# The mixer's weight halves made by GpSimd, and the stick-breaking mask made in VectorE's running product instead of by a matmul

## The chip, the cores and the metric

The kernel runs on one core of a Trainium2 chip. The metric is the device time of one execution in microseconds (us). The time given for a kernel is the median of its runs. A profiled execution gives a trace of every instruction, from which the views of the profile are drawn.

## The reference, cut to what matters

One layer of a streaming encoder, on 1024 tokens of width 1024, in float32: a half feed-forward block, a token mixer, and a second half feed-forward block, each between two RMS norms with shift, scale and gate. The change lies in the mixer, and there in its stick-breaking branch (8 heads of dimension 64) and in the projections that feed both of its branches:

```python
proj = u @ w_in                      # q, k, v of both branches, gate_A, gate_B
z = einsum('bhqd,bhkd->bhqk', qi, k) * scale
before = spos[None, :] < ti[:, None]                      # key strictly earlier than query
log_fail = where(before, log_sigmoid(-z), 0.0)
later = cumsum(log_fail, axis=3, reverse=True) - log_fail  # sum over keys between s and t
w = where(before, exp(log_sigmoid(z) + later), 0.0)
ya = einsum('bhqk,bhkd->bhqd', w, v)
```

So a key's weight is sigmoid(z) times the product of sigmoid(-z) over all later keys that are still before the query, and 0 for keys that are not before it.

## The kernel before, in words

**Split arithmetic.** Every large product is made of three TensorE matmuls in a rounded float32 format: high by high, high by low and low by high halves. The high half of an operand is a rounded copy by ScalarE, the low half is the difference of operand and high half. For a mixer weight the helper `split` (L135 to L143) does this: a DMA on SyncE's queue brings 128x1024 weights into `raw` (two buffers), ScalarE copies them to `wsH` (L141), and an engine that the caller can choose, VectorE by default, subtracts (L142) to give `wsL`. Of `wsH` and `wsL` there are four buffers each.

**The mixer's two parts.** The stick-breaking branch has four units `u` = 0 to 3, each with two heads (`par` = 0, 1), and each head has four steps `j`. A step treats two query blocks of 128 rows, `qb` = 2j and 2j+1. Block `qb` sees L = 128(qb+1) keys, so the blocks of a head are 128, 256, ... 1024 keys long. One head of four steps is called a round below: eight rounds in all. Units 4 to 7 are the four heads of the differential branch, with softmax in place of the running product.

**A step of the stick-breaking branch** (`sb_weights`, L996 to L1013). For each block and each piece of up to 512 keys: TensorE makes z by two matmuls (`qk`, L938 and L939) and, on the piece that holds the diagonal, a third one (L1005) that adds a 128x128 bfloat16 mask (0 below the diagonal, -1e30 from it on) by way of an identity matrix. ScalarE then writes sigmoid(z) to `be` (L1006) and sigmoid(-z) to `f` (L1007). VectorE runs the product backwards over the whole of `f` in one scan (L1010) and multiplies `be` by `f` one column further on (L1011). Of `f` there are two buffers, of `be` four.

**Weights times values** (`av`, L946 to L985, and `sb_out`). TensorE transposes 128x128 blocks of `be` through PSUM (L955, L956), ScalarE takes the high half `tH` (L960, L963, L965), VectorE the low half `tL` (L961, L964, L966), and TensorE multiplies both with v (L1021) into the bank `pav`. This is done for a step while the next step's z, `be` and `f` are being made.

**Filler work.** Between those pieces TensorE works on projections: classes `QJob`, `KJob`, `VJob` and `GateJob`, 48 matmuls each, a V job 192 (L813, L815, L817), dealt out by `fill` in equal shares. `advance_` (L923) loads the weights of the first two jobs of the list ahead of need (`Job.load`, L800 to L802, which calls `split`); a `VJob` needs two weight tiles and is loaded and run through where it stands (L1194). K jobs also copy their halves to the other half of the partitions on GpSimd (L866, L867), four pairs a job, which is all that GpSimd does in the mixer.

**The order.** The program is written in the order above; a list scheduler of the framework then places the instructions on the engines, by its own estimate of times. Each engine works through its list strictly in order: an instruction that waits for a semaphore holds up everything behind it on that engine.

Of the kernel before, what the change touches and what calls it, by code (L numbers as in the profile page):

```python
# [14 lines left out]
BF16 = mybir.dt.bfloat16  # L15
AF = mybir.ActivationFunctionType
ALU = mybir.AluOpType
# [3 lines left out]
P = 128  # L21
# [8 lines left out]
NEG = -1e30  # L30
# [16 lines left out]
def build(ctx, tc, A, out):  # L47
# [714 lines left out]
    pending = ffn("wg1", "wu1", "wd1", start0, pending0, steps1, lambda c: 2 if c == 1 else 5 if c < 10 else 0, steps1b, 0, lambda t: A["x"][t * P:(t + 1) * P, :], lambda t: h_dram[0][t])  # L762

    pending = mixer(locals())

    ffn("wg2", "wu2", "wd2", start_half, pending, lambda fp, psum: mod_gate(fp, psum, 2, 0.5), lambda c: 2 if c > 1 else 0, no_steps, 2, lambda t: h_dram[1][t],
# [4 lines left out]
def mixer(e):  # L771
# [4 lines left out]
    tc, nc, A, wpool, dram, U = n.tc, n.nc, n.A, n.wpool, n.dram, n.U  # L776
    V, ACT, PE, POOL, SP = nc.vector, nc.scalar, nc.tensor, nc.gpsimd, nc.sync
    split, mm3, wproj, ident = n.split, n.mm3, n.wproj, n.ident
# [7 lines left out]
    with tc.tile_pool(name="mixa", bufs=1, side="left", reuse_waits="tile") as pa, \  # L786
# [4 lines left out]
        class Job:  # L791
# [7 lines left out]

            def load(self):  # L800
                if self.w is None:
                    self.w = [split(s) for s in self.srcs]  # L802

            def step(self):
                if self.it is None:
# [104 lines left out]
        last_act = [None]  # L910
# [22 lines left out]
        def qk(q, k, i, qb, c0, c1):  # L933

            z = psum.tile([P, HALF], F32, name="z", tag="z", bufs=3)[:, :c1 - c0]
            qs = slice(qb * P, (qb + 1) * P)
            kd, kl = k
            PE.matmul(z, q[:, i, qs], kd[:, i, c0:c1], start=True, stop=False)  # L938
            last_pe[0] = PE.matmul(z, q[:, i, qs], kl[:, i, c0:c1], start=False, stop=True)  # L939
            return z  # L940

        def pieces(qb):
            L = (qb + 1) * P
            return L, [(c0, min(c0 + HALF, L)) for c0 in range(0, L, HALF)]
# [51 lines left out]
        def sb_weights(hp, par, j, q, k, fill):  # L996
            ws = []
            for qb in (2 * j, 2 * j + 1):
                L, cuts = pieces(qb)
                be = mp.tile([P, S], F32, name="be", tag="wa", bufs=4)  # L1000
                f = mp.tile([P, S], F32, name="f", tag="wb", bufs=2)
                for c0, c1 in cuts:
                    z = qk(q, k, par, qb, c0, c1)
                    if c1 == L:
                        PE.matmul(z[:, c1 - P - c0:], identb, mask_sb, start=False, stop=True, skip_group_check=True)  # L1005
                    ACT.activation(be[:, c0:c1], z, AF.Sigmoid)  # L1006
                    last_act[0] = ACT.activation(f[:, c0:c1], z, AF.Sigmoid, scale=-1.0)  # L1007
                    fill(1)
                fr = f[:, :L][:, ::-1]
                V.tensor_tensor_scan(fr, fr, fr, 1.0, ALU.mult, ALU.bypass)  # L1010
                V.tensor_mul(be[:, :L - 1], be[:, :L - 1], f[:, 1:L])  # L1011
                ws.append(be)
            return ws  # L1013

# [97 lines left out]
                list(half1)  # L1112
        n.yp.close()
        mp = stack.enter_context(tc.tile_pool(name="mixb", bufs=1, side="right", reuse_waits="tile"))
        identb = mp.tile([P, P], BF16, name="identb")
        V.tensor_copy(identb, ident)
        mask_sb = mp.tile([P, P], BF16, name="mask_sb")
        SP.dma_start(mask_sb, A["mask_sb"])
        dist = mp.tile([P, S], F32, name="dist")
        SP.dma_start(dist, A["dist"])  # L1120
        subT = mp.tile([P, 16], F32, name="subT")[:, :1]
# [26 lines left out]
        for u in range(8):  # L1148
            sb = u < 4
            if u == 4:  # L1150

                with tc.issue_after(last_act[0].ins):
                    load = ACT.add_instruction(mybir.InstLoadActFuncSet(
                        name=nc.get_next_instruction_name(), engine=ACT.engine, act_func_set_id=EXP_LN_TABLE))
                order.enter_context(tc.issue_after(load.ins if hasattr(load, "ins") else load))
# [17 lines left out]
            def fill(n):  # L1173
                seen[0] += n * wt[si]
                advance(max(0, min(total, int(total * seen[0] / points)) - done[0]))
# [8 lines left out]
            for si, (par, j) in enumerate(steps):  # L1184
                if carry is not None:
                    next(carry[0])
                if sb:
                    ws = sb_weights(u, par, j, q, k, fill)
                else:
                    ws = da_weights(u - 4, j, q, k, fill)  # L1190
                if carry is not None:
                    carry[1]()
                if si == 0 and u % 2 == 0 and u > 0:
                    vjob = VJob(u // 4, u % 4 // 2)  # L1194
                    while vjob.step():
                        pass
                it = av(ws[0], ws[1], j, fill)
                if sb:
                    carry = it, lambda par=par, j=j, it=it, u=u, vt=vjob.out, fill=fill: sb_out(u, par, j, it, vt, fill)
                else:  # L1200
                    carry = it, lambda j=j, it=it, u=u, vt=vjob.out, fill=fill: da_out(u - 4, j, it, vt, fill)
# [90 lines left out]
def _layout(inp):  # L1292
    f = lambda a: np.ascontiguousarray(a)
    a = {}
    a["x"] = f(inp["x"].reshape(S, D))
    a["cT"] = f(inp["c"].reshape(NK, P).T)

    wa = inp["w_ada"][0]
    a["wada0"] = f(wa[:, :2 * D].reshape(4, 2, P, 2, 4, 256).transpose(4, 0, 2, 1, 3, 5).reshape(4, 4, P, 2, HALF))
    a["wada"] = f(wa[:, 2 * D:].reshape(NK, P, 7, D).transpose(2, 0, 1, 3))  # L1300
    a["bada"] = f(inp["b_ada"].reshape(1, -1))
    a["badaT"] = f(inp["b_ada"].reshape(72, P).T)
    a["npreT"] = f(inp["norm_pre"].reshape(3 * NK, P).T)
    a["npost"] = f(inp["norm_post"][0])

    def cols(w, n):
        k, m = w.shape
        return f(w.reshape(k // P, P, m // n, n).transpose(2, 1, 0, 3).reshape(m // n, P, (k // P) * n))

    for i in (1, 2):  # L1310

        for n, w in (("wg", "gate"), ("wu", "up")):
            x = cols(inp[f"ffn{i}_w_{w}"][0], P).reshape(2, NPAIR, P, 2, HALF)
            a[f"{n}{i}"] = f(x.transpose(1, 2, 0, 3, 4).reshape(NPAIR, P, 4, HALF))
        x = inp[f"ffn{i}_w_down"][0].reshape(2, NPAIR, P, 2, HALF)
        a[f"wd{i}"] = f(x.transpose(1, 2, 0, 3, 4).reshape(NPAIR, P, 4, HALF))
    win = inp["w_in"][0]
    a["win"] = cols(win, P)
    wv = np.stack([win[:, 1024:1536], win[:, 2560:3072]])

    a["wv"] = f(wv.reshape(2, 2, 4, P, 2, 256).transpose(0, 4, 1, 3, 2, 5).reshape(2, 2, 2, P, 1024))
    a["wbs"] = cols(inp["w_branch_sb"][0], 256)
    a["wbd"] = cols(inp["w_branch_da"][0], 256)

    a["wo"] = f(inp["w_out"][0].reshape(4, 2, P, 2, HALF).transpose(3, 0, 2, 1, 4).reshape(2, 4, P, D))
    a["lq1"], a["lk1"] = f(inp["da_lambda_q1"]), f(inp["da_lambda_k1"])
    a["lq2"], a["lk2"] = f(inp["da_lambda_q2"]), f(inp["da_lambda_k2"])
    a["subT"] = f(inp["da_subln"].reshape(P, 1))

    import ml_dtypes  # L1330
    p, m = np.arange(P)[:, None], np.arange(P)[None, :]
    a["mask_sb"] = np.where(m < p, 0.0, NEG).astype(ml_dtypes.bfloat16)
    j = np.arange(S)[None, :] - (S - P)
    d = np.abs(p - j).astype(np.float32)
    a["dist"] = np.where((p < 64) & (j >= 64), np.float32(-NEG * 1e3), d).astype(np.float32)
    return a
# [15 lines left out]
```

## Time and profile before

| what | value |
|---|---|
| median of three runs | 2268.05 us (2264.48 to 2269.99) |
| the profiled execution's own time | 2263.8 us |
| its span, first to last instruction | 2261.9 us, so 1.9 us lie around it |
| mean granted TensorE clock | 0.988 of full speed |
| stick-breaking stage | about 780 to 1100 us of the span |
| differential stage | about 1100 to 1400 us of the span |

In the rows of the profile PE is TensorE's matmuls, PEld its weight loads, DVE is VectorE, ACT is ScalarE, POOL is GpSimd and SP is SyncE. A row of a group names line, engine, operation, output and inputs, shapes and count; behind the bar stand the busy time of all of them in us, the mean of one in ns, and how long the engine had been idle before them and for whom. A row of the timeline gives start and duration in us, and in brackets the idle time before it with what ended it. Matmuls overlap in the pipeline, so what one of them costs is read from the distance between starts, not from its duration.

### The profile page before, as it was taken

The page shows a single profiled execution, that of the slowest core. Times are in us where ns is not written, and L with a number is a line of the kernel's source. Part 1 is how long each engine was busy: PE and PEld are TensorE (multiplying, and loading weights), DVE is VectorE, ACT ScalarE, POOL GpSimd, SP SyncE. Part 2 cuts the span into 40 slices and gives each one's busy share as a digit, 9 for nine tenths or more (in the row PEclk, how much of TensorE's full clock was granted, in tenths as well). Part 3 has the DMA queues.
Part 4 walks back from the last instruction along what each step waited for, and adds up shares of the span by engine and source line. Part 5 has one row for each costly group of instructions (what it writes and reads, how often), then busy time and mean ns, then how long its engine had stood idle before and what let it go on. Part 6 is the DMA issues. An engine that isn't in the chain of part 4 may idle for free. (4 is left out here: it accounts for less than half of the span.)

```text
span 2261.9 us, 28622 instructions
## 1 busy us (share of the span) xinstructions
PE 2169.0 (96%) x10420; PEld 1792.0 (79%) x10420; DVE 1565.4 (69%) x2612; ACT 1043.2 (46%) x1882; POOL 70.2 (3%) x90
## 2 busy tenths in 40 slices
PE   5999999999999999999999999999999999999998
PEld 3777778878887877878888988788878788887886
DVE  6886877567677687576677577656886666755566
ACT  4633323325466556455545455555743232434454
POOL 1000000000000010011011010000000000000000
PEclk8899999999999999999999999999999999999999
DMA  7284874449787111110211122764475553538676
GB/s 307 79 280 164 300 258 170 147 161 314 250 276 228 60 32 45 38 48 30 62 57 59 45 96 75 236 200 139 149 242 186 177 177 135 186 117 270 210 225 217
DMA packets 137677, 364.38 MB, mean 161 GB/s; under 512 B 16704, under 2 KB 20800, under 8 KB 137536
## 3 DMA queue, kind: packets, MB, share of 16 engines
q1 hardware_dynamic: 135904, 356.79, 46.6%
q0 software_dynamic: 1632, 5.77, 0.7%
q8 instruction: 81, 1.33, 0.2%
q14 instruction: 60, 0.49, 0.1%
HBM read 272.32 MB, written 90.18 MB: 160 GB/s over the span
## 5 line engine op out<-in xcount | busy, mean ns | idle before, releaser
L813 PE MATMUL pps<-uH,wsH 128*128 128x512 f32 x512 | 209.0, 408 | 0.0
L815 PE MATMUL pps<-uL,wsH 128*128 128x512 f32 x512 | 204.5, 399 | 0.0
L817 PE MATMUL pps<-uH,wsL 128*128 128x512 f32 x512 | 203.6, 398 | 0.0
L226 DVE TENSOR_TENSOR tbL<-stg,tbH 128x512 fp32r<-128x512 f32 x154 | 105.9, 690 | 104.8 <-ACT tbH L225 104.3
L225 ACT CAST tbH<-stg 128x512 fp32r<-128x512 f32 x154 | 95.7, 621 | 156.7 <-DMA stg<-d_T 113.1
L298 PE MATMUL bank<-uH,wsH 128*128 128x512 f32 x352 | 142.2, 406 | 6.4 <-DVE uH L180 2.9
L584 PE MATMUL bankA<-tbL,sbH 128*128 128x512 f32 x352 | 138.8, 394 | 6.3 <-DVE tbL L226 6.3
L299 PE MATMUL bank<-uL,wsH 128*128 128x512 f32 x352 | 140.2, 398 | 1.4 <-POOL uL L181 1.3
L300 PE MATMUL bank<-uH,wsL 128*128 128x512 f32 x352 | 138.7, 395 | 0.0
L583 PE MATMUL bankA<-tbH,sbH 128*128 128x512 f32 x352 | 138.4, 395 | 0.1
L585 PE MATMUL bankA<-tbH,sbL 128*128 128x512 f32 x352 | 138.3, 393 | 0.1
L142 DVE TENSOR_TENSOR wsL<-raw,wsH 128x1024 fp32r<-128x1024 f32 x72 | 88.0, 1222 | 69.3 <-ACT wsH L141 68.0
L226 DVE TENSOR_TENSOR sbL<-stg,sbH 128x512 fp32r<-128x512 f32 (+1 forms) x176 | 108.2, 620 | 29.6 <-ACT sbH L225 26.9
L225 ACT CAST wsH<-s 128x1024 fp32r<-128x1024 f32 x88 | 92.0, 1049 | 72.4 <-DVE s L332 54.2
L225 ACT CAST sbH<-stg 128x512 fp32r<-128x512 f32 (+1 forms) x176 | 98.2, 565 | 52.7 <-DMA stg<-hd_A 37.6
L365 ACT COPY q<-bank 128x512 f32<-128x512 f32 x44 | 25.8, 586 | 207.1 <-PE bank L300 207.1
L817 PEld LDWEIGHTS pps<-uH,wsL 128*128 128x128 f32 x512 | 96.8, 189 | 17.4
L226 DVE TENSOR_TENSOR wsL<-s,wsH 128x1024 fp32r<-128x1024 f32 x88 | 107.2, 1219 | 3.5 <-ACT wsH L225 3.5
L813 PEld LDWEIGHTS pps<-uH,wsH 128*128 128x128 f32 x512 | 97.6, 191 | 14.3
L815 PEld LDWEIGHTS pps<-uL,wsH 128*128 128x128 f32 x512 | 97.1, 190 | 14.2
L225 ACT CAST wsH<-raw 128x1024 fp32r<-128x1024 f32 (+1 forms) x88 | 73.2, 834 | 71.5 <-PE bank L299 38.9
L583 PE MATMUL bankB<-tbH,sbH 128*128 128x512 f32 x264 | 102.8, 389 | 0.0
(247 smaller groups left out, 5941.2 us busy)
## 6 DMA issues: line engine op xcount, KB each, us to landing
wada<-in_wada SPq DMA_DIRECT2D x56, 512.0 KB, 5.2
raw<-in_wg SPq DMA_DIRECT2D x50, 512.0 KB, 6.4
raw<-in_wu SPq DMA_DIRECT2D x50, 512.0 KB, 4.5
raw<-in_wd SPq DMA_DIRECT2D x44, 512.0 KB, 4.5
stg<-hd_A SPq DMA_DIRECT2D x88, 256.0 KB, 4.2
stg<-d_S SPq DMA_DIRECT2D x88, 256.0 KB, 3.5
stg<-d_T SPq DMA_DIRECT2D x88, 256.0 KB, 3.8
d_S<-s SPq DMA_DIRECT2D x40, 512.0 KB, 2.7
```

The lines of the kernel that those rows point to most:

```text
L142: eng.tensor_sub(l, raw, h.bitcast(F32))
L225: ACT.copy(h, src)
L226: V.tensor_sub(l, src, h.bitcast(F32))
L298: PE.matmul(ps, H[:, ks], bH, start=first and k == 0, stop=False, skip_group_check=not first)
L299: PE.matmul(ps, H[:, ks], bL, start=False, stop=False, skip_group_check=not first)
L300: PE.matmul(ps, L[:, ks], bH, start=False, stop=k == 3, skip_group_check=not first)
L583: PE.matmul(ps, sH[:, ts], tH, start=first, stop=False, skip_group_check=not check)
L584: PE.matmul(ps, sH[:, ts], tL, start=False, stop=False, skip_group_check=not check)
L585: PE.matmul(ps, sL[:, ts], tH, start=False, stop=last, skip_group_check=not check)
L813: PE.matmul(ps, aH, bH, start=i == 0, stop=False)
L815: PE.matmul(ps, aH, bL, start=False, stop=False)
L817: PE.matmul(ps, aL, bH, start=False, stop=i == n - 1)
```

## The change

Two edits, both in the mixer.

1. `Job.load` passes `eng=POOL` to `split`: for all weights of Q, K, V and gate jobs (40 tiles of 128x1024) the subtraction at L142 is issued to GpSimd. The splits of the last stage of the mixer (`wbs`, `wbd`, `wo`) stay with VectorE.
2. In `sb_weights` the mask matmul goes, and with it the two constants and one DMA. ScalarE writes `f` one column to the left, and VectorE sets the last column to 0 by a memset. The running product over `f` is now two scans: the first goes over the last 128 columns (127 for the shortest block) with state = max(state * f, own), where `own` is a row of the identity matrix read backwards and the start is 0, so that the state stays 0 until the query's own column and is 1 there; the second, absent for the shortest block, goes on over the other columns as a plain product from the value that the first left. The multiplication then takes all L columns of `be` and `f` at the same place.

```diff
             def load(self):
                 if self.w is None:
-                    self.w = [split(s) for s in self.srcs]
+                    self.w = [split(s, eng=POOL) for s in self.srcs]
...
                 f = mp.tile([P, S], F32, name="f", tag="wb", bufs=2)
+                V.memset(f[:, L - 1:L], 0.0)
                 for c0, c1 in cuts:
                     z = qk(q, k, par, qb, c0, c1)
-                    if c1 == L:
-                        PE.matmul(z[:, c1 - P - c0:], identb, mask_sb, start=False, stop=True, skip_group_check=True)
                     ACT.activation(be[:, c0:c1], z, AF.Sigmoid)
-                    last_act[0] = ACT.activation(f[:, c0:c1], z, AF.Sigmoid, scale=-1.0)
+                    o = 1 if c0 == 0 else 0
+                    last_act[0] = ACT.activation(f[:, c0 + o - 1:c1 - 1], z[:, o:], AF.Sigmoid, scale=-1.0)
                     fill(1)
-                fr = f[:, :L][:, ::-1]
-                V.tensor_tensor_scan(fr, fr, fr, 1.0, ALU.mult, ALU.bypass)
-                V.tensor_mul(be[:, :L - 1], be[:, :L - 1], f[:, 1:L])
+                d0 = max(0, L - P - 1)
+                fr, own = f[:, d0:L - 1][:, ::-1], ident[:, P - (L - 1 - d0):][:, ::-1]
+                V.tensor_tensor_scan(fr, fr, own, 0.0, ALU.mult, ALU.max)
+                if d0:
+                    fr = f[:, :d0][:, ::-1]
+                    V.tensor_tensor_scan(fr, fr, fr, f[:, d0:d0 + 1], ALU.mult, ALU.bypass)
+                V.tensor_mul(be[:, :L], be[:, :L], f[:, :L])
                 ws.append(be)
             return ws
...
-        identb = mp.tile([P, P], BF16, name="identb")
-        V.tensor_copy(identb, ident)
-        mask_sb = mp.tile([P, P], BF16, name="mask_sb")
-        SP.dma_start(mask_sb, A["mask_sb"])
```

The scheduler places things anew, and the line numbers shift by four behind the edit: L961, L964 and L966 keep theirs, the scans stand at L1011 (first) and L1014 (second), the multiplication at L1015, the memset at L1002, and the matmul with v at L1025.

The first place is VectorE's list at the end of the first round of unit 0, blocks of 896 and 1024 keys. In the program's listing a scan is printed as SCALAR_TENSOR_TENSOR; the number behind a name is the buffer. Before:

```order
L1010 SCALAR_TENSOR_TENSOR f_6840<-f_6840 128x896
L1011 TENSOR_TENSOR be_6839<-be_6839,f_6840 128x895
L1010 SCALAR_TENSOR_TENSOR f_6860<-f_6860 128x1024
L961 TENSOR_TENSOR tL_6885<-trp_6879,tH_6884 128x512
L1011 TENSOR_TENSOR be_6859<-be_6859,f_6860 128x1023
L964 TENSOR_TENSOR tL_6902<-trp_6897,tH_6901 128x256
L142 TENSOR_TENSOR wsL_7385<-raw_7382,wsH_7384 128x1024
L966 TENSOR_TENSOR tL_6902<-trp_6897,tH_6901 128x128
```

And the same place after the change:

```order
L1011 SCALAR_TENSOR_TENSOR f_6841<-f_6841,ident_70 128x128
L1014 SCALAR_TENSOR_TENSOR f_6841<-f_6841 128x767
L1015 TENSOR_TENSOR be_6840<-be_6840,f_6841 128x896
L1011 SCALAR_TENSOR_TENSOR f_6862<-f_6862,ident_70 128x128
L961 TENSOR_TENSOR tL_6888<-trp_6882,tH_6887 128x512
L1014 SCALAR_TENSOR_TENSOR f_6862<-f_6862 128x895
L964 TENSOR_TENSOR tL_6905<-trp_6900,tH_6904 128x256
L1015 TENSOR_TENSOR be_6861<-be_6861,f_6862 128x1024
L966 TENSOR_TENSOR tL_6905<-trp_6900,tH_6904 128x128
```

The low half `tL` that stood behind the scan of 1024 columns now stands between the short first scan and the long second one, the next `tL` (L964) has moved ahead of the multiplication, and the weight's subtraction is gone from the list. In five of the eight rounds L961 stands between the two scans of the longest block, as here; in the other three it stands behind the second.

The second place is GpSimd's list from the end of unit 0's K copies through those of the next K job. Before, it holds nothing but the copies:

```order
L866 COPY kd_6222<-kd_6222 64x512
L867 COPY kl_6223<-kl_6223 64x512
L866 COPY kd_6920<-kd_6920 64x512
L867 COPY kl_6921<-kl_6921 64x512
L866 COPY kd_6920<-kd_6920 64x512
L867 COPY kl_6921<-kl_6921 64x512
```

After the change the subtractions stand among them:

```order
L866 COPY kd_6222<-kd_6222 64x512
L867 COPY kl_6223<-kl_6223 64x512
L142 TENSOR_TENSOR wsL_6920<-raw_6917,wsH_6919 128x1024
L142 TENSOR_TENSOR wsL_7319<-raw_7316,wsH_7318 128x1024
L142 TENSOR_TENSOR wsL_7396<-raw_7393,wsH_7395 128x1024
L866 COPY kd_6923<-kd_6923 64x512
L867 COPY kl_6924<-kl_6924 64x512
L866 COPY kd_6923<-kd_6923 64x512
L867 COPY kl_6924<-kl_6924 64x512
L142 TENSOR_TENSOR wsL_7595<-raw_7592,wsH_7594 128x1024
L866 COPY kd_6923<-kd_6923 64x512
L867 COPY kl_6924<-kl_6924 64x512
```

A K job's copies now stand behind subtractions that each wait for their weights and for ScalarE's high half.

The third place is ScalarE's list in the same tail as the first, after the change. The high half that belongs to the subtraction into `wsL_7396` above stands there, between two `tH` of the last product:

```order
L1007 ACTIVATE f_6862<-z_6871 128x512
L960 CAST tH_6887<-trp_6882 128x512
L963 CAST tH_6904<-trp_6900 128x256
L141 CAST wsH_7395<-raw_7393 128x1024
L965 CAST tH_6904<-trp_6900 128x128
L847 ACTIVATE q_6675<-pps_6811 64x512
```

It stood at the same point before, one place ahead of a Q copy. Two more high halves stand like this, both in the last round's tail; the other twelve of the stage stand earlier in a round or behind a tail's last `tH`. TensorE's list is the old one without the masks, but for a few neighbours that changed places.

More of the change, by code (lines that the diff above doesn't have):

```diff
@@ L1328, in _layout @@
     a["subT"] = f(inp["da_subln"].reshape(P, 1))
-    import ml_dtypes
-    p, m = np.arange(P)[:, None], np.arange(P)[None, :]
-    a["mask_sb"] = np.where(m < p, 0.0, NEG).astype(ml_dtypes.bfloat16)
+    p = np.arange(P)[:, None]
     j = np.arange(S)[None, :] - (S - P)
```

## The prediction

> **What bounds the kernel now.** I began with the page, went to the busy time by stage, then to the waits inside the stage that the change touches, and last to the timeline of one round of it.
>
> ```profile
> span 2261.9 us, 28622 instructions
> PE 2169.0 (96%) x10420; PEld 1792.0 (79%) x10420; DVE 1565.4 (69%) x2612; ACT 1043.2 (46%) x1882; POOL 70.2 (3%) x90
> ```
>
> TensorE is busy 96% of the span: time is gained by taking work off it or by filling its gaps, and nowhere else. The table by stage says where gaps are. Its columns are the stretch, its length, and the busy time of PE, PEld, DVE, ACT and POOL with counts, then the clock.
>
> ```profile
> 640.00:740.00 100.00, 95.06 (x438) 77.93 (x437) 72.13 (x124) 60.35 (x121) 0.00 (x0) 0.98 0.73 240
> 780.00:1100.00 320.00, 299.48 (x1708) 249.16 (x1707) 232.37 (x322) 177.88 (x399) 29.28 (x32) 0.99 0.13 40
> 1100.00:1320.00 220.00, 219.33 (x1277) 191.92 (x1276) 149.22 (x448) 102.83 (x226) 18.09 (x24) 0.99 0.18 59
> ```
>
> In the differential stage (1100 to 1320) TensorE has 0.7 us free of 220: what VectorE or GpSimd do there is under cover, and relief for them is worth nothing. In the stick-breaking stage (780 to 1100) 20.5 us are free of 320, and VectorE is busy 73%. TensorE's waits there, total, times and longest:
>
> ```profile
> PE pav L1021 <- DVE tL L961: 10.8, 7, 3.0
> PE pav L1021 <- ACT tH L965: 3.0, 4, 1.9
> PE trp L956 <- DVE be L1011: 2.1, 3, 1.1
> ```
>
> The gaps belong to VectorE's chain. The end of the first round shows how:
>
> ```profile
> 799.34 2.02 DVE L1010 TENSOR_TENSOR_SCAN f<-f 128x896 f32<-128x896 f32 x1 [1.02 <-ACT f L1007]
> 801.40 1.09 DVE L1011 TENSOR_TENSOR be<-be,f 128x895 f32<-128x895 f32 x1
> 802.41 2.28 DVE L1010 TENSOR_TENSOR_SCAN f<-f 128x1024 f32<-128x1024 f32 x1
> 804.61 0.67 DVE L961 TENSOR_TENSOR tL<-trp,tH 128x512 fp32r<-128x512 f32 x1
> 805.19 1.21 DVE L1011 TENSOR_TENSOR be<-be,f 128x1023 f32<-128x1023 f32 x1
> 806.32 0.42 DVE L964 TENSOR_TENSOR tL<-trp,tH 128x256 fp32r<-128x256 f32 x1
> 806.65 1.22 DVE L142 TENSOR_TENSOR wsL<-raw,wsH 128x1024 fp32r<-128x1024 f32 x1
> 807.79 0.28 DVE L966 TENSOR_TENSOR tL<-trp,tH 128x128 fp32r<-128x128 f32 x1
> ```
> ```profile
> 805.33 0.51 PE L1021 MATMUL pav<-tL,v 128*128 128x256 f32 x2 [1.67 <-DVE tL L961]
> 808.13 0.33 PE L1021 MATMUL pav<-tL,v 128*128 128x128 f32 x1 [0.32 <-DVE tL L966]
> ```
>
> VectorE starts this tail the moment ScalarE hands it `f`, so it was ahead until then; from 799.34 on it has no pause and TensorE waits for it. A round is thus bound by TensorE for its first blocks and by VectorE for its last two.
>
> **The change part by part**, against the profiled execution (2263.8 us with 2261.9 us of span; the median of the runs is 2268.05, 4.25 higher, and I carry the difference over).
>
> *Mask matmuls.* 64 go. A group row gives 230 ns each, but matmuls overlap, so I take distances between starts, once without a mask behind L939 and once with:
>
> ```profile
> 901.53 0.39 PE L939 MATMUL z<-kl,q 128*128 128x512 f32 x1
> 901.75 0.39 PE L813 MATMUL pps<-uH,wsH 128*128 128x512 f32 x1
> 901.98 0.40 PE L815 MATMUL pps<-uL,wsH 128*128 128x512 f32 x1
> ...
> 902.56 0.28 PE L939 MATMUL z<-kl,q 128*128 128x256 f32 x1
> 902.68 0.23 PE L1005 MATMUL z<-mask_sb,identb 128*128 128x128 bf16 x1
> 902.72 0.47 PE L813 MATMUL pps<-uH,wsH 128*128 128x512 f32 x1
> 903.03 0.39 PE L815 MATMUL pps<-uL,wsH 128*128 128x512 f32 x1
> ...
> L1005 PE MATMUL z<-mask_sb,identb 128*128 128x128 bf16 x64 | 14.7, 230 | 0.0
> ```
>
> From L939 to the second filler matmul pass 0.45 us without the mask for 512 columns (0.22 + 0.23), so about 0.34 for 256 (half of 0.22, plus 0.23); with it 0.47. One mask costs 0.13 us, most of it in the following matmul, which takes 0.31 instead of 0.23 to the next start. Taken as 0.14 (bounds 0.12, and 0.23 if nothing overlapped): 64 x 0.14 = 9.0 us. Six of a round's eight masks lie ahead of the tail, where TensorE sets the pace: 48 x 0.14 = 6.7 us gained. The other sixteen fall where VectorE does: 0.
>
> [...]
>
> *The new scans.* The first covers 128 columns, the second the rest, so only fixed cost is added:
>
> ```profile
> L1010 DVE TENSOR_TENSOR_SCAN f<-f 128x1024 f32<-128x1024 f32 x8 | 18.5, 2315 | 0.0
> L142 DVE TENSOR_TENSOR wsL<-raw,wsH 128x1024 fp32r<-128x1024 f32 x15 | 18.3, 1223 | 9.1 <-ACT wsH L141 8.1 <-PE trp L956 1.0
> L1010 DVE TENSOR_TENSOR_SCAN f<-f 128x128 f32<-128x128 f32 x8 | 3.3, 419 | 0.6 <-ACT f L1007 0.5
> ...
> L1046 DVE TENSOR_SCALAR nm<-mx 128x1 f32<-128x1 f32 x46 | 6.4, 145 | 0.3
> ```
>
> (2315 - 419) / 896 = 2.12 ns a column, so 419 - 128 x 2.12 = 148 ns are fixed; the second scan waits for the first, which costs 0.04 us as between the scan and multiplication at 801.40: 0.19 us x 56 = 10.6 us. A memset of one column is not in the trace; the nearest row is a 128x1 operation at 145 ns, bounded by 0.05 and 0.25: 64 x 0.15 = 9.6 us. VectorE gains 20 us of work in the stage. It loses 15 subtractions, 18.3 us, and the 9.1 us in which they blocked its list waiting for ScalarE. On the balance sheet it is relieved by 7 us; on the chain it isn't, since the additions all lie between `f` and `be`, and the subtractions mostly in slack. In mid-round I charge 0.3 us for a long wait of L956 per round: +2 (0 to +6); and credit -3 (-8 to 0) for subtractions that had stood in front of a waited-for `tL`.
>
> *The tails.* After: 0.42 + 0.04 + 1.75 for the first pair of scans (2.21 for 2.02), 1.08, 0.42, L961, 2.02 + 0.04, L964, 1.21. L961's result comes about 1.6 us earlier than 805.28, near 803.7, and the wait of 1.67 shrinks; but the multiplication of 1024 ends near 807.2, not 806.4 (0.2 + 0.2 of fixed cost, 0.34 for L964 that moved ahead), and behind it L966 near 807.5. TensorE reaches the L1021 at 808.13 near 807.6. In this round that saves 0.4 us, thanks to the subtraction that left; in rounds without one between L964 and L966 it loses about as much. Eight tails: +1 (-10 to +5).
>
> *GpSimd's subtraction and the shared access to SBUF.* GpSimd's own rows:
>
> ```profile
> 23.00 1.28 POOL L181 TENSOR_TENSOR uL<-u,uH 128x512 fp32r<-128x512 f32 x1 [21.69 <-DVE uH L180]
> 23.42 1.94 DVE L226 TENSOR_TENSOR wsL<-raw,wsH 128x1024 fp32r<-128x1024 f32 x1 [0.51 <-ACT wsH L225]
> ...
> 1053.14 2.29 DVE L1010 TENSOR_TENSOR_SCAN f<-f 128x1024 f32<-128x1024 f32 x1
> 1053.42 2.41 POOL L866 CAST kd<-kd 64x512 fp32r<-64x512 f32 x1 [5.26 <-ACT kd L864]
> 1055.34 0.66 DVE L865 TENSOR_TENSOR kl<-pps,kd 64x512 fp32r<-64x512 f32 x1
> ...
> L866 POOL CAST kd<-kd x32: 608/612/2413, 741.1 to 1314.8; 64x512 fp32r<-64x512 f32 x32
> ```
>
> 128x512 took 1.28 us, so 128x1024 takes at most 2.56; less one fixed part, 2.4 by estimate, against 1.22 on VectorE. And the two engines exclude each other: VectorE's 1.22 us subtraction took 1.94, ending 1.08 after GpSimd's end at 24.28; GpSimd's 0.61 us copy took 2.41, ending 0.4 after the scan's end at 1055.43. Both VectorE operations read two operands from SBUF. The scans and L1011 do too; L961 to L966 read PSUM and one operand, and run beside GpSimd (L865 did, at 1055.34).
>
> So each of the 15 subtractions of the stage waits for a scan or multiplication to end and then holds up the next by up to 2.4 us. Outside the tails VectorE has slack: 12 x 0.2. In a tail it is TensorE's time: ScalarE's order puts three high halves there (one in the first round, two in the last), 3 x about 1 after the 1.22 that VectorE saves. Together +5 (0 to +20).
>
> *Late halves.* Most weights are loaded tens of us ahead. The tight place is the V jobs:
>
> ```profile
> 1270.35 1.05 ACT L141 CAST wsH<-raw 128x1024 fp32r<-128x1024 f32 x1 [2.99 <-PE pps L815]
> ...
> 1274.29 0.28 PE L815 MATMUL vps<-wsL,uH 128*128 128x256 f32 x1
> ```
>
> High half done at 1271.40, low half needed at 1274.29 for the fifth k of the first token tile: 2.9 us for 2.4 of work. +1 (0 to +4) over the V jobs. K copies behind subtractions come up to 3 us later; the next unit's first blocks need only their first halves, and I charge nothing, +3 if that cover fails.
>
> *Elsewhere.* The four subtractions at 640 to 740 leave a VectorE busy 72%, the gap of 4.9 us there being the norm's chain: 0 (-1 to +1). Dropped constants and a DMA: 0, at the start of the mixer beside filler matmuls.
>
> Sum: -6.7 + 2 - 3 + 1 + 5 + 1 = -0.7 us: 2263.1 for the profiled execution, **2267 us** against the median.
>
> **The rivals.** A measurement of this kernel can tell about 0.3%, 6.8 us, from no change.
>
> *The tails open (faster).* The split scan lets `tL` through in five rounds, and the wait of 10.8 us halves without coming back behind L1015, because masks gone and subtractions gone shorten both sides. For it: the wait has one cause in seven places. Against: the same VectorE work ends a round. -9.0 for all masks, -5 for the waits, -3 for subtractions, +3 for the rest: 2254 us.
>
> *The lock in the chain (slower).* GpSimd's 2.4 us fall into f-to-`be` chains in most rounds, since it always gets in when a scan ends and L961 runs. 9 of 15 at 2 us are 18, less 6.7, plus 2 to 3 for the added fixed cost: +13, 2281 us. It decides from about six such collisions on. Against it: VectorE idles 27% there.
>
> [...]
>
> *No relief.* The change says that it unloads VectorE, and the added scans and memsets eat it up: with memsets at 0.25 (16 us instead of 9.6) and three quarters of the difference on the chain, -0.7 + 4.8 = +4, within no change, 2272 us.
>
> **How the numbers follow.** Forecast 0.40; no relief 0.07, also no change; tails open 0.28; lock 0.25. So faster 0.28, no change 0.47, slower 0.25. The range takes in both larger rivals' times, 2254 and 2281, and leaves out what goes beyond them, some 0.2; the forecast's own range is 2261 to 2274.
>
> **What would show it.** Right: TensorE's busy time in the stage some 15 us less in the record with a span of the stage within a few us; the subtraction on POOL at about 2.4 us alone and up to 5 when it waits; scans and L1015 with a maximum 2 us over their usual; TensorE's wait for L961 smaller, those for L964, L966 and L1015 larger. Wrong: waits for VectorE falling in total by 8 us or more (first rival), or rising by that (second); or TensorE waiting for a subtraction on POOL beyond 4 us (late halves).

## The result, and the profile after

The changed kernel takes 2291.39 us (median of 4 runs, 2288.0 to 2297.79) against 2266.94 us for the kernel before on the same chip (2264.48 to 2269.99): a ratio of 1.011, 95% interval 1.0092 to 1.0128. It is 24.5 us slower, where no change was forecast, and lies beyond the slow end of the range.

The top of the page after, and the prediction's three stretches:

```profile
span 2291.3 us, 28614 instructions
PE 2180.2 (95%) x10356; PEld 1802.4 (79%) x10356; DVE 1564.1 (68%) x2691; ACT 1043.1 (46%) x1882; POOL 166.3 (7%) x130
```
```profile
640.00:740.00 100.00, 92.42 (x413) 75.17 (x412) 71.87 (x118) 58.37 (x116) 9.96 (x4) 0.95 0.72 238
780.00:1100.00 320.00, 292.38 (x1615) 247.95 (x1614) 223.44 (x400) 164.49 (x373) 63.91 (x49) 0.96 0.13 39
1100.00:1320.00 220.00, 212.93 (x1233) 185.08 (x1232) 138.82 (x391) 103.39 (x225) 49.20 (x31) 0.98 0.17 55
```

TensorE has 64 instructions less and is still busy 11 us longer (2180.2 against 2169.0), and the granted clock of the stick-breaking stretch went from 0.99 to 0.96. Fixed windows mislead once a kernel is longer, so the stages are better cut at their own landmarks: the first score matmul of unit 0, the first of the differential stage, the first matmul of the merge. The two stages of the kernel before, and then of the kernel after (columns as above):

```profile
780.00:1092.50 312.50, 295.47 (x1692) 245.95 (x1690) 224.90 (x314) 172.38 (x391) 29.28 (x32) 0.99 0.13 41
1092.50:1416.70 324.20, 318.61 (x1802) 275.95 (x1800) 229.84 (x680) 162.84 (x352) 18.09 (x24) 0.99 0.20 66
```
```profile
787.20:1114.30 327.10, 298.23 (x1628) 251.39 (x1626) 233.04 (x417) 171.47 (x391) 62.25 (x46) 0.96 0.12 39
1114.30:1443.10 328.80, 320.94 (x1802) 276.94 (x1800) 221.67 (x661) 163.77 (x352) 66.93 (x44) 0.98 0.20 66
```

The stick-breaking stage is 14.6 us longer and the differential one 4.6, 19.2 of the 29.4 us by which the two profiled spans differ. Another 7.2 us lie ahead of 787: 2.4 of them before the first instruction that the change touches (at 645.9, 643.4 in the kernel before), where single profiles scatter (by some 5 us, as told further down), and most of the others beside the end of the first feed-forward block, where the clock of the stretch went from 0.98 to 0.95.

TensorE's longest waits after, from 740 to 1420 us:

```profile
PE trp L956 <- DVE be L1015: 11.3, 11, 2.3
PE pav L1025 <- DVE tL L961: 6.4, 6, 2.2
PE pav L1025 <- DVE tL L966: 4.7, 5, 2.3
PE pps L817 <- POOL wsL L142: 1.2, 1, 1.2
```

And one before that the list of the prediction does not have:

```profile
PE pav L1021 <- DVE tL L966: 1.9, 5, 0.7
```

The wait for L961 shrank from 10.8 to 6.4 us, as the tails were meant to do; L1015 grew from 2.1 to 11.3, and L966 from 1.9 to 4.7. TensorE hardly waits for GpSimd itself (1.2 us). Between its own landmarks the stick-breaking stage holds 24.5 us of waits for VectorE, 11.8 in the kernel before. What makes VectorE late stands in the end of the first round. VectorE, GpSimd and TensorE there, and then the clock over the same time:

```profile
812.26 2.07 DVE L1014 TENSOR_TENSOR_SCAN f<-f 128x895 f32<-128x895 f32 x1
814.25 0.40 DVE L964 TENSOR_TENSOR tL<-trp,tH 128x256 fp32r<-128x256 f32 x1
814.56 2.99 DVE L1015 TENSOR_TENSOR be<-be,f 128x1024 f32<-128x1024 f32 x1
817.48 0.28 DVE L966 TENSOR_TENSOR tL<-trp,tH 128x128 fp32r<-128x128 f32 x1
```
```profile
812.56 3.91 POOL L142 TENSOR_TENSOR wsL<-raw,wsH 128x1024 fp32r<-128x1024 f32 x1 [20.67 <-ACT wsH L141]
```
```profile
815.16 0.33 PE L1025 MATMUL pav<-tL,v 128*128 128x256 f32 x1
817.81 0.47 PE L1025 MATMUL pav<-tL,v 128*128 128x128 f32 x1 [2.32 <-DVE tL L966]
```
```profile
811.00:814.50 3.50, 2.82 (x14) 2.00 (x12) 3.47 (x5) 1.41 (x2) 1.94 (x1) 1.00 0.00 0
814.50:817.10 2.60, 0.49 (x2) 0.30 (x2) 2.60 (x2) 0.75 (x2) 1.97 (x1) 1.00 0.00 0
817.10:820.50 3.40, 2.69 (x11) 2.50 (x12) 2.95 (x8) 1.90 (x5) 0.00 (x0) 0.50 0.52 167
820.50:824.00 3.50, 3.50 (x12) 2.90 (x12) 2.72 (x9) 1.24 (x3) 0.00 (x0) 0.51 0.02 6
```

GpSimd's subtraction is handed over at 812.56, while a scan runs; it ends at 816.47, 2.14 us after the scan's end at 814.33 (alone it takes 2.40). VectorE's L964 reads PSUM and one operand from SBUF, and passes: 0.40 us, 0.42 in the kernel before. The multiplication L1015 reads two from SBUF: it takes 2.99 us instead of 1.21 and ends at 817.55, 1.08 us after GpSimd. L966 stands behind it, and TensorE waits 2.32 us. Then comes what the prediction did not have: for the next 6.9 us TensorE is granted half the clock, and matmuls of 512 columns follow each other at 0.43 to 0.57 us instead of 0.23. Such stretches of half clock, 3.4 or 6.8 us long in this stage, add up to 23.9 us; in the kernel before, the stage has a single one, of 3.4.

### The profile page after: what moved, and what is told of

Same layout as the page of the kernel before. It is cut to its first block, busy times and chain, and to the rows that moved or that the text cites. A ratio compares the mean times of both kernels' runs of the same rounds, so it can differ in the third digit from the quotient of the medians.

```text
span 2291.3 us, 28614 instructions
## 1 busy us (share of the span) xinstructions
PE 2180.2 (95%) x10356; PEld 1802.4 (79%) x10356; DVE 1564.1 (68%) x2691; ACT 1043.1 (46%) x1882; POOL 166.3 (7%) x130
## 4 chain that ended last, share of the span: by engine, by line
PE 56%; DVE 23%; DMA 11%; ACT 5%; issue 5%; SPq 0%; POOL 0%; DVEq 0%; ACTq 0%; POOLq 0%
PE bank L300 7%; PE bank L298 7%; PE bank L299 7%; DMA stg<-d_T 4%; PE pps L813 3%; PE pps L815 3%; PE pps L817 3%; DVE f L1014 2%; DVE wsL L226 2%; PE bankA L584 2%; PE bankA L583 2%; PE bankA L585 2%; DMA stg<-in_wd 2%; DVE be L1015 2%; DMA wada<-in_wada 1%
## 5 line engine op out<-in xcount | busy, mean ns | idle before, releaser
L226 DVE TENSOR_TENSOR tbL<-stg,tbH 128x512 fp32r<-128x512 f32 x154 | 110.5, 718 | 119.3 <-ACT tbH L225 118.7
L142 POOL TENSOR_TENSOR wsL<-raw,wsH 128x1024 fp32r<-128x1024 f32 x40 | 101.6, 2545 | 557.2 <-ACT wsH L141 498.0
L815 PEld LDWEIGHTS pps<-uL,wsH 128*128 128x128 f32 x512 | 98.9, 193 | 14.7
```

The costliest lines, as they stand in the source:

```text
L142: eng.tensor_sub(l, raw, h.bitcast(F32))
L226: V.tensor_sub(l, src, h.bitcast(F32))
L815: PE.matmul(ps, aH, bL, start=False, stop=False)
```

## The experiments

The theory after the result: GpSimd's 2.4 us subtractions and VectorE's operations on two SBUF operands exclude each other, in VectorE's chain, far more often than was charged. Rivals: the mask edit lengthens the chain and costs it all; or the low halves come too late. All ratios are to the kernel before on the same chip.

**The two halves of the change apart.** The first kernel is the one before with only this line changed; the second is the changed kernel with this line undone:

```
-                    self.w = [split(s) for s in self.srcs]
+                    self.w = [split(s, eng=POOL) for s in self.srcs]
```

> Only the first edit: the mixer's weight halves subtracted by GpSimd, the mask matmul kept. Lock theory (GpSimd's subtraction and VectorE's two-operand instructions shut each other out, and TensorE's clock drops after the gaps): +18 to +35 us over the kernel before, with scans and multiplications up to 2.4 us over their usual. Mask theory (the longer chain on VectorE made the loss): -3 to +4. Late-halves theory (GpSimd is merely slower and the weights come late): +18 to +35 as well, but TensorE's waits would name the subtraction on POOL.

> Only the second edit: the mask in VectorE's scans, the subtractions kept on VectorE. Lock theory: -10 to 0 us, the masks' matmuls gained and a little of it given back to the added fixed cost. Mask theory: +15 to +30. Late-halves theory: as the lock theory.

Subtractions on GpSimd alone: 2281.4 us, ratio 1.0071 (1.0056 to 1.0086), 14.7 us by the medians and 16.1 by the ratio. The mask edit alone: 2266.9 us, ratio 1.0007 (0.9996 to 1.0018). The stages of the first, and then of the second:

```profile
781.50:1102.90 321.40, 296.31 (x1691) 246.13 (x1691) 221.15 (x300) 172.56 (x391) 62.50 (x46) 0.99 0.12 40
1102.90:1431.80 328.90, 319.80 (x1802) 276.34 (x1801) 224.03 (x660) 163.49 (x352) 65.79 (x44) 0.99 0.20 66
```
```profile
781.70:1094.50 312.80, 290.24 (x1627) 244.65 (x1626) 236.23 (x431) 170.32 (x391) 24.18 (x32) 0.99 0.13 41
1094.50:1417.60 323.10, 318.31 (x1801) 275.13 (x1800) 230.15 (x681) 163.04 (x352) 18.06 (x24) 0.99 0.20 67
```

With GpSimd alone the stick-breaking stage grows by 8.9 us and the differential one by 4.7; TensorE's free time in the first (length less busy) goes from 17.0 to 25.1 us. The mask edit alone takes 5.2 us of busy time off TensorE (295.47 to 290.24) and gives it 5.6 us of new waiting (17.0 to 22.6): its gain is real and fully eaten. The mask theory falls as the cause of the loss.

Together the halves seem to cost more than their sum: 24.5 against about 15 us by the medians, 24.9 against 17.7 by the ratios. The intervals of the three ratios leave some 6 us of doubt either way on that surplus of 7 to 10 us. The rows say where it is in the profiled executions. Free time in the stage adds up: 17.0 + 8.1 + 5.6 = 30.7 would be the sum, 28.9 was measured (327.10 - 298.23). Busy time doesn't: 295.5 + 0.8 - 5.2 = 291.1 would be the sum, 298.2 was measured. The surplus of 7 us is TensorE doing the same matmuls slower, at a mean clock of 0.96 where each half alone kept 0.99. The stage has 23.9 us at half clock, each half alone 3.4. Nor is this one execution's accident: over the whole span the changed kernel's four runs had a mean clock of 0.979 to 0.983, the fourteen runs of the two halves 0.984 to 0.988.

**Which kind of GpSimd work hurts.** Nothing is moved here. Behind each of the 40 subtractions on VectorE stands useless work for GpSimd, a subtraction into the consumed `raw` in the first kernel, three memsets of it in the second:

```
+        if extra:
+            POOL.tensor_sub(raw, raw, h.bitcast(F32))
...
+            for _ in range(3):
+                POOL.memset(raw, 0.0)
```

> The kernel before with everything where it was, and behind each of the 40 subtractions a useless one on GpSimd of the same shape, reading two SBUF operands and writing into the spent raw tile; nobody waits for its result but the next load of that tile. Lock theory: +12 to +30 us, though VectorE keeps all its work and no weight is late. Mask theory and late-halves theory: 0 to +4.

> As the run with the useless subtraction, but with three memsets of the same tile in its place, which write SBUF and read nothing, for about as long in all. Lock theory, if what collides is the reading of SBUF: -3 to +5 us. If any GpSimd work collides: +12 to +30. Mask and late-halves theories: 0 to +4.

With the useless subtractions the kernel takes 2300.72 us, ratio 1.0159 (1.0138 to 1.0179); with the memsets 2268.15 us, 1.0007 (0.9998 to 1.0017). GpSimd's group rows, one from each:

```profile
L144 POOL TENSOR_TENSOR raw<-raw,wsH 128x1024 f32<-128x1024 f32 x40 | 98.9, 2473 | 545.1 <-DVE wsL L142 380.5 <-issue 132.2 <-DVE r L1052 15.1
```
```profile
L145 POOL MEMSET raw<- 128x1024 f32 x120 | 115.0, 962 | 515.6 <-DVE wsL L142 299.5 <-DMA raw<-in_win 144.5 <-issue 64.4
```

GpSimd is busy about as long with them in both, 99 and 115 us, and touches the same tile. Of the two, only the kind that reads SBUF costs (1.0159 against 1.0007). Nothing computes with these results (only the tile's next load waits for them), so the late low halves are out as the main cause too: 34 us are lost with every low half made on VectorE.

**What the mask matmuls are worth, and with what the surplus interacts.** Both kernels leave the stick-breaking mask out of the computation; the second has the subtractions on GpSimd besides.

```
-                    if c1 == L:
-                        PE.matmul(z[:, c1 - P - c0:], identb, mask_sb, start=False, stop=True, skip_group_check=True)
```

> The kernel before without its 64 mask matmuls and with nothing in their place: the stick-breaking mask is left out, so this is the price of those matmuls alone. As the prediction priced them (48 that count by 0.14 us): 2266.7 - 6.7 = 2260 us. If the mask edit gained nothing because the matmuls lay in time in which TensorE waited anyway: 2265 to 2267 us. The difference from the mask edit alone (2266.9 us) is what the running products, memsets and their waits take back: 6 to 7 us by the first, 0 to 1 us by the second.

> The kernel before with the 40 subtractions on GpSimd and without the mask matmuls, nothing in their place: the stick-breaking mask is left out. Alone, the first cost 14.7 us and the second gained 5 to 6 us; both edits of the change together cost 24.5 us, 9.6 more than the sum of their own two results. If that surplus comes from the mask matmuls being gone (less work of TensorE to cover a late VectorE, and more time at the halved clock), this kernel is slow too: 2260.4 + 24 = 2284 us. If it comes from the added scans and memsets of VectorE, which lengthen the tails into which GpSimd's subtractions fall, the two edits here simply add: 2260.4 + 14.7 = 2275 us.

Without the mask: 2260.4 us, ratio 0.9973 (0.9959 to 0.9987); with GpSimd besides: 2277.89 us, 1.005 (1.0035 to 1.0065). The stick-breaking stage of the first, then of the second:

```profile
784.80:1092.10 307.30, 288.81 (x1627) 244.34 (x1626) 223.47 (x314) 170.93 (x391) 29.03 (x32) 0.99 0.13 41
```
```profile
788.30:1107.10 318.80, 293.14 (x1627) 248.23 (x1627) 220.33 (x300) 171.49 (x391) 62.24 (x46) 0.98 0.13 40
```

The 64 matmuls cost 6.7 us of busy time and 5.2 us of stage. So the scans and memsets that replace them take back what was won, 6.5 us by the two medians and 7.7 by the two ratios. And the missing matmuls bring little of the surplus: -6.1 and +16.1 us by the ratios add up to +10.0, and +11.3 was measured, with the same 6 us of doubt. By what is left, most of it comes with VectorE's added work beside GpSimd's. The missing matmuls may have a part: in the profile of the second kernel TensorE's busy time is 3.5 us above the sum (293.14 against 288.81 + 0.84), with 13.7 us of the stage at half clock.

**Cutting the subtraction.** If VectorE waits for one instruction, shorter ones should hurt less. The first two kernels cut each subtraction into four instructions of 256 columns, in the changed kernel and in the one with GpSimd alone; the third into sixteen of 64.

```
-        eng.tensor_sub(l, raw, h.bitcast(F32))
+        n = 1 if eng is V else 4
+        for i in range(n):
+            s = slice(i * D // n, (i + 1) * D // n)
+            eng.tensor_sub(l[:, s], raw[:, s], h.bitcast(F32)[:, s])
```

> The changed kernel with each of the 40 subtractions on GpSimd cut into four instructions of 256 columns. Lock theory (a subtraction of GpSimd and an operation of VectorE that reads two operands from SBUF shut each other out for the length of one instruction): each wait becomes about a quarter, 2.4 us to some 0.65 us, so that of the 24.5 us lost some 6 to 10 stay: 2273 to 2277 us. Rival, the low halves are simply late (2.4 us against 1.2 us for the same subtraction): four pieces are together as long as one or longer by their fixed parts, so the time stays at 2291 us or rises to 2294 us. A third: GpSimd's pieces follow each other without letting VectorE in, then the longest VectorE operation stays 2 us above its usual and the time stays at 2291 us.

> The kernel before with the subtractions on GpSimd, each in four instructions of 256 columns, and the mask matmul kept. Lock theory: of the 14.7 us that the same edit cost in one piece, a quarter to a third stays: 2270 to 2272 us. Rival, late low halves: 2281 us or more.

> The changed kernel with each subtraction on GpSimd in sixteen instructions of 64 columns. From the lengths of 1024 and 256 columns (2.40 and 0.742 us) a piece takes some 0.33 us and the whole 5.3 us. If the 13.8 us that were left with four pieces are waits of VectorE for one instruction of GpSimd, they shrink with it: 5 to 9 us above the kernel before, 2271 to 2275 us. Rival, what was left is the lateness of the low halves (3.3 us in four pieces): with 5.3 us it grows, 2282 us or more.

Four pieces: 2279.37 us, ratio 1.0058 (1.0041 to 1.0075), and 2274.54 us, 1.0037 (1.0024 to 1.005). Sixteen: 2297.53 us, 1.0133 (1.0116 to 1.015). Four pieces leave 0.56 and 0.61 of the loss by the medians, more than was expected: the waits get shorter, but there are more of them. I counted VectorE's operations from 640 to 1450 us that ran beside a subtraction of GpSimd and over 0.3 us longer than usual (the 20th percentile of their line and shape): 19 with 28.8 us of excess in the changed kernel, 35 with 15.7 us in four pieces. That is 0.55 of the excess, for 0.56 of the loss. The excess itself is no price: with GpSimd alone it is as large (21 operations, 30.3 us), and the loss was 14.7 us.

Sixteen pieces refute the simple form of the theory. The stages, in sixteen pieces:

```profile
796.20:1111.70 315.50, 288.11 (x1625) 243.05 (x1625) 226.81 (x417) 170.69 (x391) 113.01 (x256) 1.00 0.13 40
1111.70:1450.50 338.80, 325.49 (x1803) 279.72 (x1801) 220.41 (x661) 163.86 (x352) 118.80 (x344) 0.97 0.20 64
```

The stick-breaking stage is within 3 us of the kernel before, but the differential one is 14.6 us longer, and 11.8 us were lost beside the end of the first feed-forward block. I took these for low halves that come too late (though beside the feed-forward block TensorE's longest wait, 8.0 us, was for VectorE's `y`, and none was for a subtraction), and put the ten subtractions whose weights are wanted at once back on VectorE:

```
-                    self.w = [split(s, eng=POOL) for s in self.srcs]
+                    self.w = [split(s, eng=POOL if len(self.srcs) == 1 and started[0] else V) for s in self.srcs]
```

> The changed kernel with sixteen pieces on GpSimd for 30 of the 40 subtractions; the ten whose weights are wanted at once are back on VectorE: those loaded beside the end of the first feed-forward block (four) and those of the value projections at the head of units 2, 4 and 6 (six). With all 40 in sixteen pieces the profiled span grew by 11.8 us beside the end of the feed-forward block, by 7.5 and 5.5 us in units 4 and 6, and by 3.1 us in the whole stick-breaking stage. If those three places are low halves that come too late (5.3 us for one, two behind each other), they lose some 20 of the 29.8 us here: 2274 to 2279 us, with units 0 to 3 still at 2 to 4 us over the kernel before. Rival, 640 short instructions of GpSimd disturb VectorE everywhere and the loss goes with their count: a quarter goes, 2289 us.

2284.64 us, ratio 1.0075 (1.0054 to 1.0095): a recovery of 13 us, where I expected some 20. Beside the feed-forward block the loss went (from 11.8 us to 0.5), but the differential stage stayed 14.0 us longer. TensorE waited there only 1.0 us for a subtraction, so lateness explains little of it. At its first place GpSimd, then VectorE and ScalarE, then TensorE's stretches:

```profile
1145.80 9.21 POOL L145 TENSOR_TENSOR wsL<-raw,wsH 128x64 fp32r<-128x64 f32 x32 [17.77 <-ACT wsH L141]
```
```profile
1150.20 3.87 DVE L1063 TENSOR_TENSOR r<-r,lam 128x1 f32<-128x1 f32 x1
1154.11 0.44 DVE L1064 TENSOR_SCALAR ex<-ex,r 128x384 f32<-128x384 f32 x1
1155.84 0.72 ACT L1057 ACTIVATE ex<-ex,nm 128x512 f32<-128x512 f32 x1 [4.71 <-DVE nm L1055]
```
```profile
1150.20:1154.10 3.90, 3.90 (x22) 3.35 (x21) 3.87 (x2) 0.82 (x2) 3.90 (x15) 1.00 0.46 137
1154.10:1158.00 3.90, 1.49 (x7) 0.86 (x6) 2.90 (x10) 1.81 (x5) 1.65 (x4) 1.00 0.47 134
```

GpSimd issues a piece every 0.29 us without a pause, 32 of them in 9.21 us. A VectorE multiplication of one column, 0.16 us in the kernel before, starts among them and ends 3.87 us later: VectorE doesn't get in between two pieces. ScalarE waits 4.71 us for VectorE; TensorE has work for as long, and then stands for 2.4 of the next 3.9 us, waiting for ScalarE. In the kernel with all 40 in sixteen pieces the same operation took up to 3.577 us, with a median of 0.160. Beside another train of the later kernel VectorE did get in between pieces: 32 of them took 11.35 us from 1099.74 on, and a multiplication of 1024 columns at 1101.17 took 1.24 us, 1.21 in the kernel before. So it did in the kernel with four pieces, which follow each other without a pause too (four in 3.25 us at 1198.55), and where none of the 35 operations took over 0.6 us more than usual; what decides that I have not found.

**The value weights.** In the changed kernel, the 8 subtractions of the value projections' weights, issued in pairs, go back to VectorE:

```
-                    self.w = [split(s, eng=POOL) for s in self.srcs]
+                    self.w = [split(s, eng=POOL if len(self.srcs) == 1 else V) for s in self.srcs]
```

> The changed kernel with the subtractions of the value projections' weights (8 of the 40, issued in pairs at the head of units 0, 2, 4 and 6, where the weights are wanted at once) back on VectorE; the other 32 stay on GpSimd. If the loss sits where two subtractions stand back to back on GpSimd beside VectorE's chain at the head of a unit, half or more of the 24.5 us goes: 2275 to 2280 us. Rival, the loss is spread over all subtractions alike: a fifth of it goes, 2286 us, and unit 0 keeps its 7.9 us.

2285.02 us, ratio 1.0081 (1.0053 to 1.011). A quarter of the loss goes for a fifth of the subtractions, and the interval allows from nothing to a half. So the loss does not sit at the pairs alone; whether it is denser there stays open.

**The memsets.** The mask edit alone, with `V.memset` of line 1002 as `POOL.memset`:

> The mask edit alone (subtractions on VectorE), with its 64 memsets of one column on GpSimd, which write and read nothing. The mask edit alone took 2266.9 us, the mask left out 2260.4 us: 6.5 us for memsets, the second scan and its hand-overs. If the memsets are a part of that, 2264 us; if, as their 59 ns suggest, they cost next to nothing and the second scan is all of it, 2266 to 2267 us.

2265.16 us, ratio 0.9991 (0.9978 to 1.0003). It overlaps the interval of the mask edit alone, so whether the memsets cost anything stays open; no kernel here that computes the reference beats the one before.

## Why the prediction was wrong, step by step

**GpSimd's term failed: "+5 (0 to +20)", and with it "-3" for the subtractions gone.** Together they stood at +2; measured alone they are +14.7 us (16.1 by the ratio). The mechanism was right, down to the single operation (2.4 us alone, up to 3.91 when waiting, a scan or multiplication up to 2 us over its usual). The count was wrong. The prediction put 3 collisions on TensorE's time, at about 1 us, and called the 12 outside the tails slack at 0.2. In the stage after, six operations of VectorE were lengthened, by 1.3 to 2.1 us each, 11.0 in all: two own-block scans at the start of units 0 and 2 and four multiplications L1015. "The lock in the chain" charged 9 at 2 us, 18 in all, for this stage, where GpSimd alone cost 8.9. That its total of 2281 us is the time of the kernel with GpSimd alone is luck: it left out the differential stage and counted the masks as a gain.

**"What VectorE or GpSimd do there is under cover" failed too.** The differential stage, at 0.7 us free of 220, was charged nothing and lost 4.6 us. A full TensorE is no slack: as the rows of the sixteen pieces show, work queued ahead of it covers a wait only until it runs out (there for 3.9 us, then TensorE stood for 2.4 of the next 3.9).

**The term of the mask was the right size, the credit for it was not.** -6.7 was forecast, -5.2 (stage) and -6.1 (ratio) measured. In busy time 64 matmuls were worth 6.7 us, 0.10 each, where the prediction had read 0.14 from its rows. But the scans and memsets, "+2 (0 to +6)", cost 6.5. The memset takes 59 ns, not 150, so the second scan and its hand-over in the chain are probably most of it; no run separates them. The waits moved as forecast: in the mask edit alone L961 fell from 10.8 to 7.5 us, and L1015 rose from 2.1 to 8.2:

```profile
PE trp L956 <- DVE be L1015: 8.2, 10, 1.2
PE pav L1025 <- DVE tL L961: 7.5, 6, 2.9
```

**A term was missing: the clock.** The halves sum to about 15 us, the change costs 24.5. In the profiled stage the surplus is TensorE's busy time at half clock, four times behind stretches of some 3.4 us, as long as the shortest records of the clock, in which it was busy for only 0.28 to 0.57 of the time: gaps of 0.83 and 2.32 us, one of 2.30, one of 1.48, three of 0.8 to 0.9. Over the whole span the mean clock went from 0.988 to 0.980, 46 us of full-speed time withheld instead of 27. The mean clocks of all runs agree: 0.987 before, 0.985 and 0.986 in the halves alone, 0.980 with both, some 9 us of full-speed time beyond the sum. That the clock causes the surplus is read from these records; no run here held the clock fixed. Part of it may be scatter: in the first 498 us, where the kernels don't differ, the profiled executions of all fourteen differ by some 5 us, and the changed kernel's stands 3.1 us behind the one before.

The length of one gap doesn't settle it in the changed kernel: a gap of 2.18 us from 1078.7 on left the clock whole, one of 1.48 us from 895.7 on did not:

```profile
1078.70:1080.90 2.20, 0.03 (x1) 0.03 (x1) 2.14 (x4) 0.52 (x2) 2.14 (x3) 1.00 0.00 0
1080.90:1084.50 3.60, 3.60 (x22) 3.24 (x23) 0.80 (x4) 1.49 (x4) 0.17 (x1) 1.00 0.00 0
895.70:897.20 1.50, 0.02 (x2) 0.01 (x1) 1.50 (x4) 0.27 (x1) 0.00 (x0) 1.00 0.00 0
897.20:899.00 1.80, 1.79 (x11) 1.52 (x12) 1.32 (x4) 1.37 (x3) 1.36 (x3) 1.00 0.00 0
899.00:902.40 3.40, 3.40 (x13) 2.80 (x12) 2.96 (x9) 1.32 (x6) 0.47 (x1) 0.51 0.08 19
```

What decides when the clock falls, no run here shows.

**The signs.** The prediction called waits for VectorE that rise by 8 us the sign of the lock; in the stage they rose by 12.7 (11.8 to 24.5), but 6.7 of that comes with the mask edit alone (18.5) and 4.5 with GpSimd alone (16.3). The 15 us that TensorE's busy time in the stage was to lose became a gain of 2.8 (295.47 to 298.23).

**The smaller terms.** Late halves +1: TensorE waited 1.2 us for a subtraction, right. "Elsewhere" 0 (-1 to +1): too small. Beside the end of the feed-forward block four operations of VectorE were lengthened, by 5.4 us together, and from the last part of that block to the mixer's first projection the record is 3.6 us longer (1.5 with GpSimd alone, 0.7 with the mask edit alone).

So, of the 24.5 us: about 15 are GpSimd's reads in VectorE's way, which the experiments show; the mask edit is nil where its terms summed to -3.7; the rest, by the records alone, is the halved clock that the two bring about together.

## What to carry to other kernels

Before moving an operation that reads SBUF to GpSimd, count VectorE's operations with two SBUF operands that can fall beside it (and those with one, as the rows below show), and price each at up to the whole length of the GpSimd instruction (here subtractions that take 2.40 us alone lengthened six of them in the stick-breaking stage by 1.3 to 2.1 us, and the one below by 2.23); an engine that looks idle, as GpSimd did at 3% busy, is not a free one if its instructions hold up those on the chain. Cutting the instruction is no sure cure: four pieces left 0.56 of the loss, sixteen brought it back. And in a kernel like this one, with TensorE busy 95%, a new gap of some 2 us can cost more than itself: behind some of them, not all, the matmuls of the next 3.4 to 6.9 us ran at half speed.

## What the runs showed of the hardware that was not expected

- GpSimd's subtraction of 128x1024 takes 2.40 us alone, 128x256 0.742 and 128x64 0.32, one every 0.29 us in a train; VectorE's memset of one column takes 59 ns.
- A VectorE operation with a single operand in SBUF waited for GpSimd as well. In the changed kernel, usual time 0.29 us, beside a subtraction from 1214.52 to 1216.92:

```profile
1214.52 2.40 POOL L142 TENSOR_TENSOR wsL<-raw,wsH 128x1024 fp32r<-128x1024 f32 x1 [14.68 <-ACT wsH L141]
1214.55 0.08 DVE L1044 DVE_READ_ACCUMULATOR2_ANT mx<- 128x1 f32 x1
1214.55 2.52 DVE L1089 TENSOR_SCALAR ms<-ms 128x256 f32<-128x256 f32 x1
```

  In the kernel with the useless memsets (ratio 1.0007) the same operation took up to 1.571 us against a median of 0.292:

```profile
L1088 DVE TENSOR_SCALAR ms<-ms x16: 288/292/1571, 1153.5 to 1423.4; 128x256 f32<-128x256 f32 x16
```
- A train of short GpSimd instructions kept a 0.16 us operation of VectorE waiting: it took 3.87 us.
